# The weight products of a decoder trunk issued as 256-column halves instead of 512 columns

## The chip, the cores and the metric

One core of one Trainium2 chip runs the kernel. The metric is the device time of one launch in microseconds (us), where lower is better. A profile is the record of one execution, and its span runs from the first to the last recorded instruction.

## The reference

Two layers of a decoder trunk work on 256 tokens of width 2048, all in float32. Layer 0 mixes tokens by stick-breaking attention and gated linear attention, layer 1 by a diagonal state-space layer (S5) with a gated output projection. Each layer ends in a SwiGLU feed-forward block of inner width 5632. Cut to what matters here, the time is that of the large weight products, marked `@`:

```python
def sb_gla_mixer(h, w_in, ...):            # layer 0
    proj = (h @ w_in)                      # 2048 -> 6160
    ...
    return jnp.concatenate([o_sb, o_gla], axis=-1) @ w_out   # 2048 -> 2048

def s5_mixer(h, ..., w_glu):               # layer 1
    ...
    val, gate = jnp.split(y @ w_glu, 2, axis=-1)             # 2048 -> 4096
    return val * jax.nn.sigmoid(gate)

def swiglu_ffn(h, w_ffn_in, w_ffn_out):    # both layers
    gate, up = jnp.split(h @ w_ffn_in, 2, axis=-1)           # 2048 -> 11264
    return (jax.nn.silu(gate) * up) @ w_ffn_out              # 5632 -> 2048
```

## The kernel before, in words

A weight matrix is cut into blocks of 512 output columns, and each block into k-tiles of 128 rows. The 256 tokens are two token blocks (`tb` 0 and 1) of 128. For a product, TensorE holds 128 features of 128 tokens as its stationary operand (128x128, loaded by an instruction of its own, LDWEIGHTS, which the profile lists under PEld) and streams the 512 weight columns of one k-tile past it into a PSUM tile of 128 tokens by 512 columns, which is one whole PSUM bank.

Float32 accuracy is kept by splitting. A weight chunk `wraw` is copied on ScalarE (ACT) to the rounded format fp32r as `whi`, and VectorE (DVE) subtracts that from the original and leaves the rest in `wlo`. The activations are split likewise into a high and a low part (`xh` and `xl`; `ah` and `al` in the second feed-forward product; halves of `og` and `os` in the output projection of layer 0). Each k-tile then takes three products, high by high (L203), high by low (L204) and low by high (L205), which all add into the same bank. L203 and L204 follow each other with the same stationary operand, and each has its own load. An accumulation over 16 k-tiles is 48 such products; the first has `start=True`, the last `stop=True`.

`products` issues the products of two k-tiles (one "unit") for one token block. `linear` walks over the column blocks, takes the next split unit from the weight stream `ws`, and calls `products` for both token blocks. `pairwise` does the same for two column blocks at once. Between units, `pump` lets background work (attention, the S5 preparation) issue a little work on VectorE and ScalarE. Its budget counts estimated VectorE and ScalarE time alone, so what TensorE is given does not change where it stops. Order on each engine is the order in which the code is written.

A part of the GLU weights is used unsplit in plain float32 by L198 (32 products of 512 columns, each recorded as two passes with a load each). Smaller TensorE work that the prediction reads from: L734 multiplies fp32r activations of 256 columns by a stationary operand of only 16 columns (48 products in a row); L810, plain float32 products of 128 columns (two recorded passes each); L480, transposes of 128 columns; L1233, the S5 preparation's products with a 32-column stationary operand; L1490, the S5 output's small products.

Of the kernel before, what the change touches and what calls it, by code (L numbers as in the profile page):

```python
# [159 lines left out]
class Kern:  # L160
# [31 lines left out]
    def products(self, ps, acts, tb, u, part):  # L192
        hi, lo = part
        mm = self.nc.tensor.matmul
        if lo is None:
            for kk in range(2):
                k = 2 * u + kk
                mm(ps, lhsT=self.whole[k][:, tb * 128:(tb + 1) * 128], rhs=hi[:, kk, :], start=(k == 0), stop=(k == len(acts) - 1))  # L198
            return
        for kk in range(2):  # L200
            k = 2 * u + kk
            xh, xl = (a[:, tb * 128:(tb + 1) * 128] for a in acts[k])
            mm(ps, lhsT=xh, rhs=hi[:, kk, :], start=(k == 0), stop=False)  # L203
            mm(ps, lhsT=xh, rhs=lo[:, kk, :], start=False, stop=False)  # L204
            mm(ps, lhsT=xl, rhs=hi[:, kk, :], start=False, stop=(k == len(acts) - 1))  # L205


    def linear(self, blocks, acts, evac, opening=None, mid=None, hooks=None, spare=None):
# [497 lines left out]
    def gla(self, rs):  # L706
# [86 lines left out]
        yield from self.need(256)  # L793
        mix = self.got.pop(256)
        yield from products(S[1], mix, mix, 0, 128, lambda o, p: nc.vector.tensor_copy(o, p))
        for li, b in enumerate((64, 32, 16, 8, 4, 2, 1)):
            yield from self.need(2 * b + 1)
# [805 lines left out]
```

## Time and profile before

| what | value |
|---|---|
| time, median of 3 runs | 2205.46 us (2204.25 to 2205.67) |
| time of the profiled execution | 2204.35 us |
| its span | 2202.6 us |
| granted TensorE clock, mean | 0.996 |
| TensorE matmuls (PE), busy | 2159.6 us, 98% of the span, 10672 recorded |
| TensorE weight loads (PEld), busy | 1741.4 us, 79%, 10672 recorded |
| VectorE (DVE), busy | 1319.5 us, 60% |
| ScalarE (ACT), busy | 974.3 us, 44% |
| HBM | 207 GB/s over the span |

A matmul's recorded duration is not what it costs in a stream: the next one starts before it has ended. What a product costs is the time from its start to the start of the next one, called its spacing below. A load's recorded duration likewise overlaps the matmul ahead of it, and where loads are close together, the next load as well.

### The profile page before, as it was taken

What the parts mean: (1) busy time and instruction counts of PE and PEld (TensorE: products, weight loads), DVE (VectorE), ACT (ScalarE), POOL (GpSimd) and SP (SyncE); (2) the same over time, 40 slices, a digit from 0 to 9 for tenths busy, and PEclk for the clock granted to TensorE, in tenths of its full rate; (3) what the DMA queues carried; (4) which work ended last, traced back from release to release, by engine and by line L of the source; (5) the groups of instructions that cost most, each with busy time, mean ns of one, the idle gap of its engine ahead of it and who ended that gap; (6) DMA issues with size and microseconds to landing.
All of it is one profiled execution on the core that took longest, in us unless ns stands there. A gap on an engine that the chain in (4) does not pass through costs nothing.

```text
span 2202.6 us, 26942 instructions
## 1 busy us (share of the span) xinstructions
PE 2159.6 (98%) x10672; PEld 1741.4 (79%) x10672; DVE 1319.5 (60%) x1913; ACT 974.3 (44%) x1222; POOL 7.1 (0%) x14
## 2 busy tenths in 40 slices
PE   8999999999999999999998899999999999999998
PEld 6888888788888888777786678878888888888886
DVE  4675654667777877875456864564544454444445
ACT  5454544463454444334344254464434444433433
POOL 0000000000000000000000000000000000000000
PEclk9999999999999999999999999999999999999999
DMA  7554454555687778988769865645555555555553
GB/s 230 171 176 156 159 173 155 206 190 175 202 268 236 241 221 267 300 275 275 238 214 349 305 209 185 213 170 176 195 183 191 191 173 190 174 206 174 191 172 134
DMA packets 261742, 457.42 MB, mean 208 GB/s; under 512 B 22736, under 2 KB 66016, under 8 KB 260720
## 3 DMA queue, kind: packets, MB, share of 16 engines
q1 hardware_dynamic: 260896, 450.99, 62.0%
q0 software_dynamic: 720, 4.72, 0.6%
q8 instruction: 83, 1.36, 0.2%
q14 instruction: 43, 0.35, 0.0%
HBM read 425.26 MB, written 30.41 MB: 207 GB/s over the span
## 4 chain that ended last, share of the span: by engine, by line
PE 94%; DVE 3%; ACT 1%; DMA 1%; issue 0%; SPq 0%; DVEq 0%; ACTq 0%
PE lin L203 29%; PE lin L205 29%; PE lin L204 29%; PE lin L198 1%; PE big L480 1%; DVE h L65 1%; DVE X L65 0%; PE big L810 0%; DVE wlo L65 0%; ACT xh L65 0%; PE big L1233 0%; PE big L205 0%; PE big L204 0%; PE big L203 0%; DVE xl L65 0%
## 5 line engine op out<-in xcount | busy, mean ns | idle before, releaser
L65 DVE TENSOR_TENSOR wlo<-wraw,whi 128x1024 fp32r<-128x1024 f32 x705 | 850.3, 1222 | 591.1 <-ACT whi L65 588.8
L65 ACT CAST whi<-wraw 128x1024 fp32r<-128x1024 f32 x705 | 725.3, 1051 | 670.7 <-PE lin L205 609.2
L203 PE MATMUL lin<-whi,xh 128*128 128x512 f32 x1984 | 790.6, 398 | 3.4 <-ACT xh L65 3.4
L204 PE MATMUL lin<-wlo,xh 128*128 128x512 f32 x1984 | 785.1, 396 | 3.0 <-DVE wlo L65 2.9
L205 PE MATMUL lin<-whi,xl 128*128 128x512 f32 x1984 | 784.9, 396 | 0.9 <-DVE xl L65 0.9
L203 PEld LDWEIGHTS lin<-whi,xh 128*128 128x128 f32 x1984 | 374.9, 189 | 91.2 <-ACT xh L65 4.0
L204 PEld LDWEIGHTS lin<-wlo,xh 128*128 128x128 f32 x1984 | 374.8, 189 | 90.4 <-DVE wlo L65 6.0
L205 PEld LDWEIGHTS lin<-whi,xl 128*128 128x128 f32 x1984 | 374.5, 189 | 88.7 <-DVE xl L65 2.2
L203 PE MATMUL lin<-whi,ah 128*128 128x512 f32 x680 | 270.0, 397 | 0.0
L205 PE MATMUL lin<-whi,al 128*128 128x512 f32 x680 | 268.9, 395 | 0.0
L204 PE MATMUL lin<-wlo,ah 128*128 128x512 f32 x680 | 268.9, 395 | 0.0
L203 PEld LDWEIGHTS lin<-whi,ah 128*128 128x128 f32 x680 | 128.1, 188 | 30.8 <-issue 1.2
L205 PEld LDWEIGHTS lin<-whi,al 128*128 128x128 f32 x680 | 128.1, 188 | 30.3
L204 PEld LDWEIGHTS lin<-wlo,ah 128*128 128x128 f32 x680 | 128.1, 188 | 30.0
L65 DVE SCALAR_TENSOR_TENSOR a<-lin,rs,a 128x512 f32<-128x512 f32 x44 | 31.0, 746 | 67.3 <-PE lin L205 67.3
L65 ACT ACTIVATE a<-lin,rs 128x512 f32<-128x512 f32 x44 | 27.9, 684 | 92.2 <-PE lin L205 92.2
L65 DVE TENSOR_TENSOR yg<-lin,yg 128x512 f32<-128x512 f32 x30 | 19.9, 687 | 52.1 <-PE lin L205 52.1
L65 ACT ACTIVATE junk<-yg 128x512 f32<-128x512 f32 x24 | 15.2, 632 | 74.1 <-DVE yg L65 74.1
L65 ACT CAST ah<-big 128x1024 fp32r<-128x1024 f32 x22 | 22.3, 1015 | 56.2 <-PE big L480 56.2
L65 DVE TENSOR_TENSOR al<-big,ah 128x1024 fp32r<-128x1024 f32 x22 | 26.9, 1223 | 17.1 <-ACT ah L65 17.1
L65 ACT ACTIVATE xh<-big,gT 128x128 fp32r<-128x128 f32 (+1 forms) x80 | 24.3, 394 | 21.5 <-PE big L337 16.9
L65 DVE SCALAR_TENSOR_TENSOR xl<-big,gT,xh 128x128 fp32r<-128x128 f32 (+1 forms) x80 | 24.5, 371 | 13.6 <-ACT xh L65 13.6
(323 smaller groups left out, 1287.1 us busy)
## 6 DMA issues: line engine op xcount, KB each, us to landing
wraw<-w_ffn_in SPq DMA_DIRECT2D x176, 1024.0 KB, 5.1
wraw<-w_ffn_out SPq DMA_DIRECT2D x88, 1024.0 KB, 5.5
wraw<-w_in SPq DMA_DIRECT2D x47, 1024.0 KB, 5.0
wraw<-w_glu SPq DMA_DIRECT2D x32, 1024.0 KB, 5.7
wraw<-w_out SPq DMA_DIRECT2D x16, 1024.0 KB, 5.1
e_d<-ed SPq DMA_DIRECT2D x64, 144.0 KB, 5.9
et<-e_d SPq DMA_DIRECT2D x16, 576.0 KB, 6.3
win_d<-win SPq DMA_DIRECT2D x32, 256.0 KB, 6.6
```

Of the source, the lines that this page charges most:

```text
L65: return f(*a, **k)
L198: mm(ps, lhsT=self.whole[k][:, tb * 128:(tb + 1) * 128], rhs=hi[:, kk, :], start=(k == 0), stop=(k == len(acts) - 1))
L203: mm(ps, lhsT=xh, rhs=hi[:, kk, :], start=(k == 0), stop=False)
L204: mm(ps, lhsT=xh, rhs=lo[:, kk, :], start=False, stop=False)
L205: mm(ps, lhsT=xl, rhs=hi[:, kk, :], start=False, stop=(k == len(acts) - 1))
L480: nc.tensor.transpose(p[:, tb, i, :], a[:, tb, i * 128:(i + 1) * 128], self.ident)
```

## The change

Each product of L203 to L205 that is neither the first nor the last of its accumulation is issued as two matmuls of 256 columns, one into each half of the same PSUM bank, with the same stationary operand and each with a load of its own. The first product (which clears the bank's state) and the last one stay at 512 columns. The unsplit path (L198) is left as it is. The order of products, the arithmetic and the instructions of the other engines stay the same.

```diff
         for kk in range(2):
             k = 2 * u + kk
             xh, xl = (a[:, tb * 128:(tb + 1) * 128] for a in acts[k])
-            mm(ps, lhsT=xh, rhs=hi[:, kk, :], start=(k == 0), stop=False)
-            mm(ps, lhsT=xh, rhs=lo[:, kk, :], start=False, stop=False)
-            mm(ps, lhsT=xl, rhs=hi[:, kk, :], start=False, stop=(k == len(acts) - 1))
+            first, last = k == 0, k == len(acts) - 1
+            for x, w, start, stop in ((xh, hi, first, False), (xh, lo, False, False), (xl, hi, False, last)):
+                for c in (slice(0, 512),) if start or stop else (slice(0, 256), slice(256, 512)):
+                    mm(ps[:, c], lhsT=x, rhs=w[:, kk, c], start=start, stop=stop)
```

In the instruction order of TensorE, the first unit of the program (two k-tiles of token block 0, then the same of token block 1, ahead of the next transposes) reads before the change, with the source line, the operation, output and inputs, and the output's partitions by columns:

```order
10 L203 MATMUL lin_109<-whi_122,xh_91 128x512
11 L204 MATMUL lin_109<-wlo_123,xh_91 128x512
12 L205 MATMUL lin_109<-whi_122,xl_92 128x512
13 L203 MATMUL lin_109<-whi_122,xh_91 128x512
14 L204 MATMUL lin_109<-wlo_123,xh_91 128x512
15 L205 MATMUL lin_109<-whi_122,xl_92 128x512
16 L203 MATMUL lin_109<-whi_122,xh_91 128x512
```

And in the changed kernel, where "x2" at a row's end is two such matmuls in a row:

```order
10 L206 MATMUL lin_109<-whi_122,xh_91 128x512
11 L206 MATMUL lin_109<-wlo_123,xh_91 128x256 x2
12 L206 MATMUL lin_109<-whi_122,xl_92 128x256 x2
13 L206 MATMUL lin_109<-whi_122,xh_91 128x256 x2
14 L206 MATMUL lin_109<-wlo_123,xh_91 128x256 x2
15 L206 MATMUL lin_109<-whi_122,xl_92 128x256 x2
16 L206 MATMUL lin_109<-whi_122,xh_91 128x512
```

Nothing trades places: rows 11 to 15 are doubled where they stand, and row 16 is the first product of token block 1. Over the whole program 8544 products of 512 columns become 364 of 512 and 16,360 of 256, so 8180 are split. The orders of VectorE, ScalarE, GpSimd and the DMA queue are the same but for line numbers.

## The prediction

> **What bounds the kernel now.** I read the page's engine shares, the slices, the chain of work that ended last and the costliest groups, in that order.
>
> ```profile
> PE 2159.6 (98%) x10672; PEld 1741.4 (79%) x10672; DVE 1319.5 (60%) x1913; ACT 974.3 (44%) x1222; POOL 7.1 (0%) x14
> PE   8999999999999999999998899999999999999998
> PEclk9999999999999999999999999999999999999999
> PE 94%; DVE 3%; ACT 1%; DMA 1%; issue 0%; SPq 0%; DVEq 0%; ACTq 0%
> L203 PE MATMUL lin<-whi,xh 128*128 128x512 f32 x1984 | 790.6, 398 | 3.4 <-ACT xh L65 3.4
> L204 PE MATMUL lin<-wlo,xh 128*128 128x512 f32 x1984 | 785.1, 396 | 3.0 <-DVE wlo L65 2.9
> L205 PE MATMUL lin<-whi,xl 128*128 128x512 f32 x1984 | 784.9, 396 | 0.9 <-DVE xl L65 0.9
> L203 PEld LDWEIGHTS lin<-whi,xh 128*128 128x128 f32 x1984 | 374.9, 189 | 91.2 <-ACT xh L65 4.0
> ```
>
> TensorE is busy in nearly every slice at the full granted clock, the chain is 94% TensorE, and the products wait for almost nothing: 3.4, 3.0 and 0.9 us in total ahead of 1984 of each kind. So the time is the count of products times their spacing, and whatever the change does to the spacing goes straight to the end. The recorded 396 ns is not that spacing, since starts lie closer. The spacing comes from the starts in a quiet stretch of the second layer's feed-forward block (start us, duration us, engine, line):
>
> ```profile
> 1799.68 0.39 PE L205 MATMUL lin<-whi,xl 128*128 128x512 f32 x1
> 1799.91 0.39 PE L203 MATMUL lin<-whi,xh 128*128 128x512 f32 x1
> 1799.91 0.19 PEld L204 LDWEIGHTS lin<-wlo,xh 128*128 128x128 f32 x1
> 1800.14 0.39 PE L204 MATMUL lin<-wlo,xh 128*128 128x512 f32 x1
> 1800.14 0.19 PEld L205 LDWEIGHTS lin<-whi,xl 128*128 128x128 f32 x1
> ...
> 1805.95 0.39 PE L205 MATMUL lin<-whi,xl 128*128 128x512 f32 x1
> ```
>
> From the first to the last row are 27 products in 6.27 us: 232.2 ns each. The load of the next product starts with the present product and is over (0.19 us) before the next one starts, so it is hidden.
>
> **What the change adds.** 8180 products are split, each into two matmuls and two loads. The other 364 and the plain float32 ones keep their spacing. The whole sum is therefore 8180 x (2T - 232.2 ns), where T is the spacing of a 256-column fp32r matmul with a 128-column stationary operand. No row of before has just that, so T must be bounded.
>
> First, the row with the right width. L734 streams 256 fp32r columns, but its stationary operand has only 16 columns:
>
> ```profile
> 48.80 0.28 PE L734 MATMUL big<-xl,wlr_split 128*16 128x256 f32 x1
> ...
> 50.84 0.28 PE L734 MATMUL big<-xl,wlr_split 128*16 128x256 f32 x1
> 51.05 0.61 PE L738 MATMUL big<-dg,cst 128*16 128x128 f32 x4
> L734 PEld LDWEIGHTS big<-xh,wlr_split 128*16 128x16 f32 x32 | 3.0, 95 | 1.8 <-ACT wlr_split L65 0.9 <-DVE wlr_split L65 0.4
> ```
>
> Every third product is of this name, so 18 lie between the two: 2.04 us / 18 = 113.3 ns. That is less than half of 232.2 (116.1), and it is the lower bound for T.
>
> Second, can a 128-column load keep up at that pace? L810, plain float32 with two passes of 128 columns each, shows loads of full size at nearly the same pace:
>
> ```profile
> 118.02 1.99 PEld L810 LDWEIGHTS big<-qd,de 128*128 128x128 f32 x16
> 118.25 1.95 PE L810 MATMUL big<-qd,de 128*128 128x128 f32 x16
> L810 PE MATMUL big<-qd,de 128*128 128x128 f32 x112 | 13.6, 275 | 0.0
> 864.07 0.64 PE L1233 MATMUL big<-et 128*32 128x128 f32 x16
> 864.65 0.50 PE L203 MATMUL lin<-whi,xh 128*128 128x512 f32 x1
> 864.99 0.39 PE L204 MATMUL lin<-wlo,xh 128*128 128x512 f32 x1
> ```
>
> The 16 matmuls take (1.95 - 0.275) / 15 = 112 ns each, with 16 loads in the same time, although a load is recorded at nearly 190 ns: loads overlap one another. What a load takes by itself is seen at 864.65, where L203 could not have its load hidden: it is followed after 0.34 us instead of 0.232, so 0.108 us more. A load of about 108 ns under a product of at least 113 still fits, with 5 ns to spare instead of over 120. I cost the second load at nothing; the cover is the product's own stream, and if it is gone, the price is rival three's.
>
> Third, what does a matmul cost besides its columns? Plain float32 gives two widths with full-size loads:
>
> ```profile
> 1251.64 2.74 PE L198 MATMUL lin<-wraw,y 128*128 128x512 f32 x6
> L198 PE MATMUL lin<-wraw,y x64: 592/593/697, 1249.4 to 1281.8; 128*128 128x512 f32 x64
> 619.81 0.93 PE L480 MATMUL big<-ident,a 128*128 128x128 f32 x7
> L480 PE MATMUL big<-ident,a 128*128 128x128 f32 x176 | 22.8, 273 | 0.0
> ```
>
> 512 columns: (2.74 - 0.593) / 5 = 429.4 ns. 128 columns: (0.93 - 0.273) / 6 = 109.5. The difference, 319.9 ns over 384 columns, is 0.833 ns a column, which leaves 109.5 - 106.6 = 2.9 ns per matmul. Half of that column rate would give an fp32r product 512 x 0.4165 + 2.9 = 216.1 ns. It takes 232.2, so 16.1 ns are unexplained. L734 has 113.3 - 109.5 = 3.8 ns of the same kind. The question is what the 16.1 ns go with:
> - with the columns of this kind of product: T = (232.2 - 2.9)/2 + 2.9 = 117.6;
> - with widths over 256, in the bank or in the stream: T = 113.3, as L734;
> - with each matmul of a full-size stationary operand: T = 109.5 + 16.1 = 125.6.
>
> That the load under the product is to blame is unlikely. The product at 863.75 has no load under it:
>
> ```profile
> 863.75 0.40 PE L205 MATMUL lin<-whi,xl 128*128 128x512 f32 x1
> 864.07 0.38 PEld L1233 LDWEIGHTS big<-et 128*32 128x32 f32 x16 [0.36 <-PE lin L204]
> ```
>
> Its successor starts 0.32 us later, and that of the last L734, likewise a change of shape, after 0.21 (50.84 to 51.05). The difference, 0.11 us by times rounded to 0.01, stands against 119 ns between the two spacings in full streams (232.2 - 113.3). So the excess is there without the load.
>
> I take the first, T = 117.6: a column cost is what the long streams suggest, and it lies between the others. By it a split adds just one fixed part, 2.9 ns: 8180 x 2.9 = 24 us. From the profiled execution's 2204.35 us (span 2202.6 and 1.75 around it; 1.1 under the median of the runs) that is 2228. Its own range is from T = 116.1 (nothing) to T = 118.9, where the 5.6 ns that 232.2 has over two L734 spacings goes to each matmul: 8180 x 5.6 = 46 us. That makes 2204 to 2250.
>
> The other edits have one answer each. Instructions: 8180 more matmuls and loads must be fetched and issued. L1490 shows that pairs can be issued much faster than needed, 192 in 4.8 us or 25 ns each, so I cost issue at nothing:
>
> ```profile
> L1490 PE MATMUL lin<-e,X 64*32 64x128 f32 x192 | 4.8, 334 | 2.6 <-DVE X L65 2.6
> q8 instruction: 83, 1.36, 0.2%
> ```
>
> Fetching takes 0.2% of the DMA engines now and perhaps twice that after. VectorE and ScalarE are issued the same work at 60% and 44%; if products got 2% faster they would be as far from the bound as now. The tail after the last product doesn't change, since that one stays at 512.
>
> **The skill against the trace.** The rows above say a 512-column pair costs 232.2 ns and that a 256-column one with a small load costs 113.3. The Trainium skill, page "TensorE: Matmul & The Clock Gate", section "Back-to-back issue gap", speaks against the change: it says that in a stream of load and matmul pairs both set the spacing, with about 81 ns at 128 columns and 131 ns at 512. A straight line between these gives, as an estimate from that page, 98 ns at 256, so a split would add 65 ns, 8180 of them 530 us, and the time would be about 2735. The trace agrees neither with its 131 ns (232.2 here) nor with its 98 (113.3), so I give it no more than rival three's chance.
>
> **The rivals.**
> One, faster: the extra time sits in streams longer than 256 columns, and the width decides, not the stationary operand. T = 113.3, a split saves 5.6 ns, 46 us in all: 2158. For it: L734 is the only fp32r row of that width, and its 48 products keep 113.3 without an exception in the stretch shown. Against: its stationary operand and output have 16 columns and partitions instead of 128. It decides as soon as T is below 116.1.
>
> Two, much slower: the 16.1 ns are paid per matmul with a full stationary operand, by changing the weights or starting the output. T = 125.6, a split adds 19 ns, 155 us: 2360. For it: L734, with an eighth of the stationary columns, shows only 3.8 of it. Against: plain float32 matmuls with full stationary operands show 2.9 ns in all.
>
> Three, very slow: the load comes out from under the product, because with 5 ns to spare it doesn't overlap the next one in this format as it does in L810. At worst T is the recorded load, 189 ns, a split adds 146 ns, 1.19 ms: 3397. Against it is L810's pace of 112.
>
> Four, nothing: the chip treats 512 columns as two halves anyway, T = 116.1 and the second load hidden: 2204.
>
> **How the numbers follow.** Within 0.2%, 4.4 us, a measurement of this kernel hardly tells a change from none. The column cost has 0.42 (0.05 of it at the end within 0.2%), rival one 0.31, rival two 0.20, rival three 0.03, rival four 0.04. Faster is rival one: 0.31. Same is 0.05 + 0.04 = 0.09. Slower is 0.37 + 0.20 + 0.03 = 0.60. Leaving rivals two and three out would leave out 0.23, so the range takes in two: from rival one with 8 us of slack, 2150, to rival two with 5, 2365. The likeliest case's own range is 2204 to 2250.
>
> **What the profile after would show.** The spacing of 256-column starts decides everything: 117 to 118 for the column cost, 113 for rival one, 125 or more for rival two, near 190 for rival three. PE and PEld must count 8180 more each, 18,852. Loads should still start with a product and be followed by their own product one spacing later. Waits for `whi` and `wlo` should stay at a few us; if they grow, issue or the conversions became the bound. I would be wrong if T depended on the load after all, or if the two halves of a bank got in each other's way, which no row of before shows.

## The result, and the profile after

The changed kernel takes 2238.95 us (median of 4 runs, 2236.84 to 2240.12) against 2204.94 before: 1.0153 times as long, 95% interval 1.0136 to 1.0171, or 34 us more. The profiled span is 2238.0 us against 2202.6.

From the page of the changed kernel (engine shares, instruction queue, chain, product groups):

```profile
span 2238.0 us, 43302 instructions
PE 2197.0 (98%) x18852; PEld 2145.9 (96%) x18852; DVE 1320.4 (59%) x1913; ACT 974.4 (44%) x1222; POOL 7.1 (0%) x14
q8 instruction: 147, 2.41, 0.4%
PE 94%; DVE 3%; ACT 1%; DMA 1%; issue 0%; SPq 0%; DVEq 0%; ACTq 0%
L206 PE MATMUL lin<-whi,xh 128*128 128x256 f32 (+1 forms) x3845 | 801.0, 287 | 2.3 <-ACT xh L65 2.3
L206 PE MATMUL lin<-wlo,xh 128*128 128x256 f32 x3968 | 795.9, 282 | 2.4 <-DVE wlo L65 2.3
```

TensorE is as full as before and waits as little as before (2.3 and 2.4 us ahead of the groups). VectorE and ScalarE did the same work. The 8180 further matmuls and loads are there; the loads now fill 96% of the span instead of 79%. So the 35.4 us of span went into spacing: 35.4 / 8180 = 4.3 ns a split, and T = (232.2 + 4.3) / 2 = 118.3 ns on average. A quiet stretch of the feed-forward block (start us, duration us, engine, line; x2 is two in a row):

```profile
1829.85 0.40 PE L206 MATMUL lin<-whi,xl 128*128 128x256 f32 x2
1830.09 0.40 PE L206 MATMUL lin<-whi,xh 128*128 128x256 f32 x2
1830.33 0.40 PE L206 MATMUL lin<-wlo,xh 128*128 128x256 f32 x2
...
1833.65 0.40 PE L206 MATMUL lin<-whi,xh 128*128 128x256 f32 x2
```

From the first to the last row are 32 matmuls in 3.80 us, 118.8 ns each. The row that had carried rival one is no longer what it was either. This is L734's code (L735 in the changed kernel), which the change doesn't touch:

```profile
48.27 0.28 PE L735 MATMUL big<-xl,wlr_split 128*16 128x256 f32 x1
...
51.43 0.28 PE L735 MATMUL big<-xl,wlr_split 128*16 128x256 f32 x1
```

27 matmuls in 3.16 us are 117.0 ns each, against 113.3 before. The change moves no tile, so a spacing that differs here for the same instructions with the same operands is not set by the instruction's shape alone, nor by that and the place of its operands.

### The profile page after: what moved, and what is told of

The parts are those of the page before. It is cut to its first block, busy times and chain, and to the rows that moved or that the text cites. A ratio compares the mean times of both kernels' runs of the same rounds, so it can differ in the third digit from the quotient of the medians.

```text
span 2238.0 us, 43302 instructions
## 1 busy us (share of the span) xinstructions
PE 2197.0 (98%) x18852; PEld 2145.9 (96%) x18852; DVE 1320.4 (59%) x1913; ACT 974.4 (44%) x1222; POOL 7.1 (0%) x14
## 4 chain that ended last, share of the span: by engine, by line
PE 94%; DVE 3%; ACT 1%; DMA 1%; issue 0%; SPq 0%; DVEq 0%; ACTq 0%
PE lin L206 87%; PE big L206 1%; PE lin L198 1%; PE big L481 1%; DVE X L65 0%; PE big L811 0%; ACT xh L65 0%; PE big L1234 0%; DVE wlo L65 0%; DVE h L65 0%; DVE xl L65 0%; DMA wraw<-w_in 0%; PE big L338 0%; PE big L735 0%; ACT whi L65 0%
## 5 line engine op out<-in xcount | busy, mean ns | idle before, releaser
L206 PE MATMUL lin<-whi,xh 128*128 128x256 f32 (+1 forms) x3845 | 801.0, 287 | 2.3 <-ACT xh L65 2.3
L206 PE MATMUL lin<-wlo,xh 128*128 128x256 f32 x3968 | 795.9, 282 | 2.4 <-DVE wlo L65 2.3
L206 PE MATMUL lin<-whi,xl 128*128 128x256 f32 (+1 forms) x3842 | 794.2, 286 | 0.9 <-DVE xl L65 0.9
L206 PEld LDWEIGHTS lin<-wlo,xh 128*128 128x128 f32 x3968 | 618.5, 189 | 12.2 <-DVE wlo L65 4.1
L206 PEld LDWEIGHTS lin<-whi,xh 128*128 128x128 f32 x3845 | 599.1, 189 | 9.0 <-ACT xh L65 3.0
L206 PEld LDWEIGHTS lin<-whi,xl 128*128 128x128 f32 x3842 | 594.9, 189 | 1.5 <-DVE xl L65 1.5
L206 PE MATMUL lin<-whi,ah 128*128 128x256 f32 (+1 forms) x1314 | 272.7, 286 | 0.0
L206 PE MATMUL lin<-wlo,ah 128*128 128x256 f32 x1360 | 271.6, 281 | 0.0
L206 PE MATMUL lin<-whi,al 128*128 128x256 f32 (+1 forms) x1314 | 271.2, 285 | 0.0
L206 PEld LDWEIGHTS lin<-wlo,ah 128*128 128x128 f32 x1360 | 212.2, 189 | 3.0
```

The costliest lines, as they stand in the source:

```text
L206: mm(ps[:, c], lhsT=x, rhs=w[:, kk, c], start=start, stop=stop)
```

## Experiments

**One: bursts, in which only the matmul's shape varies.** 48 matmuls in a row behind the kernel's last write, with `xh` moving and `xl` stationary.

```diff
...
+    burst("fullwide", 128, full)          # stationary columns, cuts of the 512
+    burst("fewwide", 16, full)
+    burst("fullhalves", 128, halves)
+    burst("fewhalves", 16, halves)
+    burst("fullhalf", 128, half)          # the same half each time
+    burst("widezero", 128, full, zero=True)
...
+    burst("col384", 128, [slice(0, 384)]) # and 320, 192, 128
...
+    burst("twobankhalf", 128, half, banks=True)
...
```

> The kernel before, with bursts of fp32r matmuls added behind its last write, where VectorE, ScalarE and the weight transfers are idle: 48 in a row into one PSUM tile, of which only columns, stationary size, data or banks change; nothing reads their sums. Column theory (2.9 ns a matmul plus 0.448 ns a column, load hidden): 512 columns 232 ns apart, 256 columns 117.6, 384 columns 175, 320 columns 146, and a stationary operand of 16 columns changes nothing (232 and 117.6). Matmul theory (a full stationary operand costs each matmul 5.6 ns over L734's rate): 232 and 118.9 with 128 stationary columns, but 227 and 113 with 16. Load theory (the load under a product takes time from it): as the matmul theory with 16 columns, and slower the more loads there are for the columns. Both halves of one bank getting in each other's way would show as halves slower than the same half over and over, or than halves in two banks. For 192 and 128 columns the product is shorter than the load of 108 ns, so that all theories expect 108 to 112 there, if loads overlap as in L810. With zeros as moving data all three expect no change.

Its timeline, one row a burst (start, length in us):

```profile
2206.29 11.04 PE L577 MATMUL fullwide<-xh,xl 128*128 128x512 f32 x48
2217.63 11.26 PE L577 MATMUL fewwide<-xh,xl 128*16 128x512 f32 x48
2229.19 5.92 PE L577 MATMUL fullhalves<-xh,xl 128*128 128x256 f32 x48
2235.41 5.76 PE L577 MATMUL fewhalves<-xh,xl 128*16 128x256 f32 x48
2241.47 5.92 PE L577 MATMUL fullhalf<-xh,xl 128*128 128x256 f32 x48
2247.69 11.05 PE L577 MATMUL widezero<-zero,xl 128*128 128x512 f32 x48
2265.26 8.48 PE L577 MATMUL col<-xh,xl 128*128 128x384 f32 x48
2274.05 7.21 PE L577 MATMUL col<-xh,xl 128*128 128x320 f32 x48
2281.55 5.50 PE L577 MATMUL col<-xh,xl 128*128 128x192 f32 x48
2287.37 5.47 PE L577 MATMUL col<-xh,xl 128*128 128x128 f32 x48
2293.19 11.20 PE L577 MATMUL midwide<-xh,xl 128*96 128x512 f32 x48
2316.71 5.92 PE L577 MATMUL twobankhalf<-xh,xl 128*128 128x256 f32 x48
2323.79 7.07 PE L577 MATMUL plainhalves<-xh,xl 128*128 128x256 f32 x32
```

The rows of col are 384, 320, 192 and 128 columns. Each length but the last row's is 47 spacings and the last matmul's recorded duration (0.39 us at 512 columns, 0.28 at 256, between them by width). That gives 226.6 ns for 512 columns, 173.3 for 384, 146.8 for 320 and 119.9 for 256; 192 and 128 both come out near 111. The four widths from 512 down to 256 lie on one line of 0.417 ns a column and 13.3 ns a matmul. None of the theories said that: 512 columns are faster here than in the streams of the kernel, 256 slower, and the fixed part is neither 2.9 nor 5.6 ns. In such a burst a split costs 2 x 119.9 - 226.6 = 13.2 ns. With 16 stationary columns it is 231.1 and 116.6 (and 230.0 for 512 columns with 96), so a small stationary operand makes 512 columns slower and 256 faster, which ends the matmul theory. Halves in the same place, in turn, or in two banks cost the same 5.92 us, and zeros change nothing: neither the bank nor the data matters. Below some 235 columns, an estimate from these numbers ((111 - 13.3) / 0.417), the load's floor of about 111 ns holds. The last row is plain float32 in halves, 16 matmuls of two passes each, with full-size loads: (7.07 - 0.38) / 31 = 215.8 ns a pass, where the prediction's price for that format gives 256 x 0.833 + 2.9 = 216.2. So the 2.9 ns hold for plain float32, and fp32r has 13.3.

**Two: only the products with the low weights split.**

```diff
-            mm(ps, lhsT=xh, rhs=lo[:, kk, :], start=False, stop=False)
+            for c in (slice(0, 256), slice(256, 512)):
+                mm(ps[:, c], lhsT=xh, rhs=lo[:, kk, c], start=False, stop=False)
```

> Only the products with the low weights (L204; 2848, a third) are split. The change cost the profiled span 35.4 us over 8180 splits, 4.3 ns each. If a split has a price of its own (column and matmul theory), 2848 x 4.3 = 12 us more than before, about 2217. If the price came only where many splits follow one another, because the loads then run without a break (load theory), less than half of that, under 2211.

2199.19 us, 0.9974 times before (0.9963 to 0.9984): 6 us faster. No theory expected a gain; the load theory's bound of 2211 holds it only in form. A split has no fixed price of its own: these 2848 gain 2 ns each.

**Three: uneven cuts, to test the cover of the second load.**

```diff
-                for c in ... else (slice(0, 256), slice(256, 512)):
+                for c in ... else (slice(0, 384), slice(384, 512)):
```

> As the change, but with cuts at 384 and 128 columns instead of 256 and 256: the same number of matmuls, loads and columns. If only columns and matmuls count, the time is that of the change, 2239. If the load is hidden by the product it runs under and its own 108 to 112 ns are the floor, the matmul with 128 columns cannot take its 60 ns: it takes 110, and a split costs 175 + 110 - 232 = 53 ns, 8180 of them 430 us, about 2635. If the floor of a load were its recorded 189 ns, 175 + 189 - 232 = 132 ns, about 3285.

2642.45 us in one run, near the 2635 of the load's floor. In its timeline, x2 is a matmul of 384 and one of 128 columns:

```profile
1831.25 0.45 PE L206 MATMUL lin<-whi,xl 128*128 128x384 f32 x2
1831.54 0.45 PE L206 MATMUL lin<-whi,xh 128*128 128x384 f32 x2
1831.82 0.45 PE L206 MATMUL lin<-wlo,xh 128*128 128x384 f32 x2
1832.11 0.45 PE L206 MATMUL lin<-whi,xl 128*128 128x384 f32 x2
```

0.86 us for three splits are 287 ns each, 55 more than an unsplit product (53.5 a split over the whole program); 53 were expected. So the load in this format overlaps the next one as in L810, its pace is about 110 ns, and 256 columns just cover it.

**Four: what sets the spacing, addresses or sequence.** More bursts of 512 and 256 columns with everything else idle, now with one operand shifted in SBUF, with the kernel's own weight buffers, and with the kernel's order of three.

```diff
+    burst("control", lambda r: [(st(xl, r), mv(xh, r))], n=48)
+    burst("movp32", lambda r: [(st(xl, r), mv(xh, r, 32))], n=48)       # moving operand 128 bytes further
+    burst("movp16", lambda r: [(st(xl, r), mv(xh, r, 16))], n=48)       # 64 bytes
+    burst("stap32", lambda r: [(st(xl, r, 256, 32), mv(xh, r))], n=48)  # stationary operand further
+    burst("stap16", lambda r: [(st(xl, r, 256, 16), mv(xh, r))], n=48)
+    burst("weight", lambda r: [(st(xl, r), wt(hi, r))], n=48)           # moving: the kernel's whi buffers
+    burst("three", three, n=16)                                         # the kernel's order
...
```

> The kernel before with a second set of bursts behind its last write, again nothing read from their sums. In e1, 512 columns came 226.7 ns apart in a burst against 232.4 in the kernel, and 256 columns 120.0 against 118.4 in the changed kernel. Two theories for the difference. Addresses: the spacing depends on where in SBUF the moving and the stationary operand lie relative to each other, since transfers and the other engines did not matter; then shifting one of them by 16 or 32 columns (64 or 128 bytes), or using the kernel's own weight buffers, moves the control's 226.7 to 230 to 234. Sequence: it depends on which operands follow each other; then the shifted bursts and the plain weight burst stay at 226.7, and only the kernel's order of three (high by high, high by low, low by high) gives 232.4, and another order of the three something else. If all bursts stay at 226.7 and 120, the cause is the work beside them (VectorE, ScalarE, weight transfers), which the bursts lack.

Its timeline; the profile leaves numbers out of names, so the two rows of movp are 128 and 64 bytes, and those of stap likewise, in this order:

```profile
2204.12 11.04 PE L575 MATMUL control<-xh,xl 128*128 128x512 f32 x48
2215.45 11.36 PE L575 MATMUL movp<-xh,xl 128*128 128x512 f32 x48
2227.11 11.15 PE L575 MATMUL movp<-xh,xl 128*128 128x512 f32 x48
2238.56 11.30 PE L575 MATMUL stap<-xh,xl 128*128 128x512 f32 x48
2250.16 11.36 PE L575 MATMUL stap<-xh,xl 128*128 128x512 f32 x48
2307.17 11.36 PE L575 MATMUL weight<-bwhi,xl 128*128 128x512 f32 x48
2318.82 0.40 PE L575 MATMUL three<-bwhi,xh 128*128 128x512 f32 x1
...
2328.11 0.40 PE L575 MATMUL three<-bwlo,xh 128*128 128x512 f32 x1
...
2330.43 0.40 PE L575 MATMUL threehalf<-bwhi,xh 128*128 128x256 f32 x2
...
2335.94 0.41 PE L575 MATMUL threehalf<-bwhi,xl 128*128 128x256 f32 x2
...
2336.65 0.39 PE L575 MATMUL other<-bwhi,xh 128*128 128x512 f32 x1
...
2347.10 0.39 PE L575 MATMUL other<-bwhi,xh 128*128 128x512 f32 x1
...
2354.43 5.86 PE L575 MATMUL weighthalf<-bwhi,xl 128*128 128x256 f32 x48
2360.58 5.85 PE L575 MATMUL movp32half<-xh,xl 128*128 128x256 f32 x48
2366.74 5.86 PE L575 MATMUL stap32half<-xh,xl 128*128 128x256 f32 x48
```

By the same reckoning the control takes 226.6 ns, the shifts 233.4, 228.9, 232.1 and 233.4, and the weight buffers 233.4. The built program places `whi` and `wlo` 128 bytes past `xh` and `xl` within 512 bytes, which is the first shift. The kernel's own order of three, from 2318.82 to 2328.11 with 40 products, takes 232.3, as in the kernel, with no weight transfer and no other engine at work. Another order of the three products takes the same (`other`: 45 products in 10.45 us, 232.2 ns), which the sequence theory had excluded. So the address theory holds for 512 columns: 232 instead of 227 ns is a matter of where moving and stationary operand lie. Shifts by whole multiples of 512 bytes, which the control burst has between its matmuls, did no harm.

With 256 columns a shift works the other way: the last three rows give 118.5 to 118.7 ns, against the 119.9 of experiment one. But the kernel's order of three in halves takes 119.8 (`threehalf`: 46 matmuls in 5.51 us), and its other order 118.7, although the offset is the same. So the offset is not the whole account of the halves.

**Five and six: one other product split, and two of three.**

```diff
 # five: only low by high                # six: both products with the high weights
-  ... if start or stop else ...           -  ... if start or stop else ...
+  ... if start or stop or x is xh else ...  +  ... if start or stop or w is lo else ...
```

> Only the product with the low activations (L205) is split, but not the last of an accumulation: 2666 splits. If a split costs a fixed price in every place, as the 4.3 ns of the change would have it, 2205 + 11 = 2216; e2 already spoke against that (2199). If one split product among three is cheap because its neighbours of 512 columns give back what it costs, the same as e2, about 2199. If it was the product with the low weights that mattered, because it shares its stationary operand with the product before it, more than before again, 2210 to 2216.

> The two products with the high weights are split and the one with the low weights is not: 5332 splits. By the price of the change, 2205 + 23 = 2228. If prices just add, the change's 34 us less e2's gain of 6 leaves 40 us for these two: 2245. If 512-column neighbours give back what a split costs, something between one and all split, 2199 to 2239, about 2210.

2201.42 us, 0.9986 times before (0.9976 to 0.9995), and 2202.10, 0.9988 (0.9979 to 0.9997). Five came out nearest to the 2199 that was expected if one split among three is cheap; six came out below each single figure that was expected, but inside the span of 2199 to 2239. In the three choices tried (two, five, six), with one or two of three products split, the kernel is 3 to 6 us faster than before; only with nearly all split is it 34 us slower. The prices don't add. In the sixth, the three products of a k-tile follow each other so:

```profile
1829.96 0.40 PE L206 MATMUL lin<-whi,xl 128*128 128x256 f32 x2
1830.19 0.39 PE L206 MATMUL lin<-whi,xh 128*128 128x256 f32 x2
1830.42 0.39 PE L206 MATMUL lin<-wlo,xh 128*128 128x512 f32 x1
...
1832.04 0.39 PE L206 MATMUL lin<-whi,xl 128*128 128x256 f32 x2
```

Three k-tiles take 2.08 us, nine products of 231 ns, although six of them are split and have a matmul more. With one product of the three left whole, two halves cost no more than one whole.

The row of L734 (L735 here) is back at its old spacing in five:

```profile
46.69 0.28 PE L735 MATMUL big<-xl,wlr_split 128*16 128x256 f32 x1
...
49.75 0.28 PE L735 MATMUL big<-xl,wlr_split 128*16 128x256 f32 x1
```

27 matmuls in 3.06 us are 113.3 ns each. In the ten profiles of this case its second half stands at 113.3 ns in four (the kernel before, two, four and five) and at 117.1 in the other six. Its code is the same in all of them, and up to experiment six no tile of the kernel is moved. What decides between the two spacings is not known.

**Seven: the kernel before, with operands lined up.** The tiles are moved so that moving and stationary operands have the same place within 512 bytes. No instruction changes.

```diff
-        self.new_x()
         self.hss = [pool.tile([128, 4], F32, tag="hss", name=f"hss_{tb}", bufs=4) for tb in range(2)]
+        self.new_x()
...
+        mp.tile([128, 48], F32, name="pad")
         self.cst = mp.tile([128, C_PAR - C_TRI], F32, name="cst")
...
+                fp.tile([128, 48 if layer else 32], F32, name=f"pad{layer}")
                 ah = fp.tile([128, 16, 256], F32R, tag="ah", name=f"ah{layer}")
```

> The kernel before with its 512-column products, but with tiles moved in SBUF: a 128-byte group of small tiles goes ahead of xh and xl, and pads of 128 or 192 bytes ahead of og, os, ah and al, so that within 512 bytes the moving weights (whi, wlo) and the stationary activations begin at the same place; before, they began 128, 192 or 320 bytes apart. Instructions and their order stay. Address theory: all split products take the 226.7 ns of e1's and e4's bursts with equal offsets instead of 232.5, some 8500 x 5.8 = 49 us, so 2156. If the kernel's spacing came from its other work or the order of its products, no change, 2205.

2158.22 us, 0.9790 times before (0.9776 to 0.9803): 47 us faster where 49 were expected, and the fastest version of all. Its products:

```profile
1799.62 0.39 PE L203 MATMUL lin<-whi,xh 128*128 128x512 f32 x1
1799.85 0.39 PE L204 MATMUL lin<-wlo,xh 128*128 128x512 f32 x1
...
1806.42 0.39 PE L203 MATMUL lin<-whi,xh 128*128 128x512 f32 x1
```

30 products in 6.80 us are 226.7 ns each. Here `xh` and `xl` have come to the place that `whi` and `wlo` have within 512 bytes; in the control bursts both operands lay at the old place of `xh` and `xl`. Both give 226.7, so it is the place of the two operands relative to each other that counts.

**Eight: the change, with operands lined up.** The same edit on the changed kernel.

> The changed kernel with the same tiles moved. Address theory: with equal offsets, bursts of 256 columns came 120.0 ns apart, so a split costs 2 x 120.0 - 226.7 = 13.3 ns here instead of 4.3, and 8180 of them 109 us over e7, which makes about 2265 (26 us slower than the change itself). If alignment only speeds up, or the split keeps its 4.3 ns, e7 plus 35: about 2191.

2260.54 us, 1.0251 times before (1.0237 to 1.0265); 2265 were expected.

```profile
1799.95 0.40 PE L206 MATMUL lin<-wlo,xh 128*128 128x256 f32 x2
1800.19 0.41 PE L206 MATMUL lin<-whi,xl 128*128 128x256 f32 x2
...
1803.79 0.41 PE L206 MATMUL lin<-whi,xl 128*128 128x256 f32 x2
```

32 matmuls from the first row to the last in 3.84 us are 120.0 ns each. Lined up, the same split costs 102 us (2260.54 - 2158.22), 12.5 ns each, three times what it cost before, and the changed kernel itself is 22 us slower lined up than not (26 were expected).

## Why the prediction was right, and where not

- **What bounds the kernel**: right. TensorE stayed the chain, waits stayed under 1 ns a product, and all of the difference is spacing. The other engines played no part; the bursts have the kernel's spacing without them.
- **The size**: T = 117.6 was forecast and 118.3 measured, 24 us against 34. The time lies in the likeliest case's own range.
- **The second load stays covered**: right, with the cover as thin as said. Experiment three took it away and paid 55 ns a split; the load's pace is about 110 ns, not its recorded 189. That a covered load costs nothing at all is not shown: every matmul here has a load of its own, so no run tells what part of the 13.3 ns is the load's.
- **The step that failed is what the 16.1 ns go with.** The forecast charged them to the columns and took the fixed part of 2.9 ns over from plain float32. With lined-up operands the line through four widths of fp32r has 13.3 ns fixed and 0.417 ns a column, so a split costs 12.5 to 13.3 ns there. The columns cost just the half rate of 0.4165 that the prediction began with, and its 16.1 ns are, to within 0.1, a larger fixed part (13.3 - 2.9 = 10.4) and the operands' offset (232.2 - 226.6 = 5.6). In the kernel before, the offset adds that to a 512-column product and takes a little from a 256-column matmul (118.3 against 120.0 in the kernels; in the bursts 118.6 against 119.9, though 119.8 in the kernel's own order). The sum of these made a split look cheap. That 2.9 came near 4.3 is luck: the column cost behind it isn't there.
- **Rival one** (113.3 as L734) is false, and its row was the weakest evidence: the same instructions took 117.0 in the changed kernel, and either value in other programs.
- **Rival two** had the mechanism, a fixed part for each matmul, but it isn't bound to a full stationary operand (116.6 with 16 columns, no more than 3.3 below a full one), and it put all of the 16.1 ns into it. The price of a split, 12.5 to 13.3 ns where operands are lined up, was 4.3 here.
- **The halves of one bank** don't hinder each other: same half, halves in turn and two banks are equal to 0.01 us in 48.
- **The Trainium skill's spacing** ("TensorE: Matmul & The Clock Gate", "Back-to-back issue gap": 81 and 131 ns in a stream) doesn't agree with any burst here; 512 columns never took less than 226.6 on average, and the 98 estimated from it for 256 stand against 116.6 or more. The formula that the Trainium skill gives in the same section for a matmul by itself, N / 2.4 + 2.5 ns for N columns, is the nearer one: its slope is the 0.417 ns a column measured here, though the fixed part here is 13.3 ns and not 2.5.

What stays open is why the offset matters, why one or two split products among three cost nothing while all three cost 4.3 ns each, and what puts the same stream, as L734's, at one of two spacings. No run here shows the cause of any of the three.

## What to carry to other kernels

When TensorE is full and its spacing is a few per cent over its best burst, measure bursts of the same instruction before changing instructions: the place of its two operands was worth more here (47 us) than any of the cuts tried (6 us at best). A fixed part that was read from one format, 2.9 ns from plain float32, may not hold in another, 13.3 in fp32r. A row of the same shape from another place in the program is a weak bound: L734 took 113.3 or 117.1 ns with its operands in the same place, so compare such a row in several programs before building on it. And a split has a floor, the next load: at 192 columns of this format the load set the pace, at 256 it no longer did, and by the estimate above the border is near 235.

## What was unexpected of the hardware

With one operand moved by 64 or 128 bytes, nothing else changed and the other engines and the weight transfers idle, 512-column fp32r matmuls went from 226.6 to between 228.9 and 233.4 ns apart. One and the same stream of matmuls, L734's, settled at 113.3 ns in four programs and at 117.1 in six. In lined-up bursts the four widths follow 13.3 ns + 0.417 ns a column to within 0.2 ns. And a smaller stationary operand, 16 columns instead of 128, made 512-column matmuls slower: 231.1 against 226.6.
